# SSD scan of a hybrid decoder step: the samples' token parts read four-fold from memory on 128 rows, in place of three-fold copies turned by TensorE

## The chip, the cores and the metric

The kernel runs on one core of one Trainium2 chip. The metric is device time in microseconds of one execution of the whole program, which is one inference step of two decoder layers for 512 prompt tokens and 8 samples of 8 tokens each. An execution outside the profiler takes a little more than the span that the profile shows, since the span runs from the first to the last instruction.

## What is computed

Layer 0 is a Conformer and sliding-window attention mixer, layer 1 a Mamba-2 mixer, and each is followed by a convolutional FFN. The change lies in layer 1, in the chunked scan. Cut to what matters, the reference is:

```python
def ssd_scan(x, dt, a, bm, cm, h0):          # x: tokens, heads, 64; bm, cm: tokens, 4 groups, 128
    ...
    acum = jnp.cumsum(dtc * a.reshape(g, r), axis=2)
    decay = jnp.exp(jnp.where(causal, diff, -jnp.inf))
    cb = jnp.einsum('bclgn,bcsgn->bclsg', cc, bc)
    w_intra = (cb[..., None] * decay * dtc[:, :, None])
    y_diag = jnp.einsum('bclsgr,bcsgrp->bclgrp', w_intra, xc)
    decay_end = jnp.exp(acum[:, :, -1:] - acum)
    states = jnp.einsum('bclgn,bclgr,bclgrp->bcgrpn', bc, decay_end * dtc, xc)
    ...                                       # h = chunk_decay * h + states, over the chunks
    y_off = jnp.einsum('bclgn,bcgrpn,bclgr->bclgrp', cc, h_prev, jnp.exp(acum))
```

For the prompt there are four chunks of 128 tokens that start from a zero state. For the samples each of the 8 sequences is one chunk of 8 tokens that starts from its own state `h0`, and the new state of every sequence is an output: new state = decayed old state + (B of its 8 tokens) times (x of its 8 tokens, times `dt` and `decay_end`). That last product, for the samples, is what the change concerns.

## The kernel before

**Layout.** Activations lie channels by tokens: 576 columns, of which 512 are the prompt's and the last 64 the samples'. Every weight product is split in three (high weight times high and low activation, low weight times high activation: lines 160 to 162 in `mm3`), on halves of 288 columns. A weight block of 128 x 1024 comes by one DMA into one of three buffers `wr` (line 141), ScalarE rounds it to `wh` (line 150), VectorE forms the rest `wl` (line 151); one block feeds 48 such products. I call these products the wide products.

**Slots.** Working tiles come from a list of 48 + 11 equal slots (`S`, `free`, `NSLOT`, `EXTRA`). A tile gets the slot that has been free longest, so a new tile waits until the last user of its slot is done, whatever engine or DMA that was.

**The scan.** `mix1` runs `ssd(g)` for four groups g = 0 to 3, of eight heads and one B and one C each. I call them scan 0 to scan 3. `ssd` is a generator; `run(main, side)` interleaves its steps with weight units (gate columns z, B and C of the next group, the output projection of the group before), spread over n = 30 steps. The final order on each engine is made by a scheduler when the program is built, and from then on each engine executes its own list in order and waits where an operand or a slot isn't ready. All DMAs are issued by SyncE (queue SP), in order too.

The steps of one scan, with their lines:

- B of the prompt is turned to tokens by channels on TensorE (line 951, `btok` line 953).
- **The samples' state operands** (lines 955 to 988). B and the four x tiles of the group are copied by ScalarE into tiles `r3` in which the samples' 64 columns stand as two halves of 32, each three times over (line 958). TensorE turns them to 96 rows: two turns for B (line 966), eight for x (line 979). From B, ScalarE and VectorE make `bp` (rounded; the third copy holds the rest) and `b3` (lines 968 to 973); from x, VectorE makes `xf`, times `dd3`, a tile of `dt * decay_end` made three-fold once by a product with `sel3` (lines 923 to 928), and `x3` (lines 983 to 985). Three copies on 96 rows make one matmul yield high*high + low*high + high*low.
- C times B of each chunk, masked (`pc`, `pcs`, `cbm`, lines 991 to 999).
- x is turned to tokens by channels, times `dt`: `xdt`, four prompt chunks and one tile of the 64 sample tokens (lines 1002 to 1013).
- The chunk states (`pst`, `hst`, lines 1015 to 1029); the last goes out as `ssm_p` (line 1030).
- Then for each pair of heads t = 0 to 3: `carried` (line 1056: rows `ea2` of the cumulated decays from memory `acd`, product `py`), two `decays` (line 1044: 256 KB `acb` from `acd`, four ScalarE ops, one exponential, one VectorE product), `outputs` (line 1069: product `yp`).
- `load`, `begin` and `finish` (lines 1088 to 1123): the samples' old states `h0` come in, are multiplied by C (`pyo`) and decayed, and `finish` adds `b3` times `x3` (line 1118) and writes the new states.

Of the kernel before, what the change touches and what calls it, by code (L numbers as in the profile page):

```python
# [40 lines left out]
for _name, _w in (  # L41
    ("ident", 128), ("m32", 32), ("prot", 128), ("blk2", 2), ("amask", 256), ("smask", 2 * 192),
    ("tri", 128), ("tris", 64), ("bmat", 64), ("bsel", 8), ("selx", 256), ("selm", 128),
    ("sel3", 192), ("bsel3", 4),
):
    CV[_name] = _n
    _n += _w
# [2 lines left out]

class Builder:
    NSLOT = 48
    EXTRA = 11

    def __init__(self, nc, tc, d, stack):
        self.nc, self.tc, self.d = nc, tc, d
# [747 lines left out]
    def mix1(self):  # L804
        nc, d = self.nc, self.d
# [53 lines left out]
        W = 160  # L859
        pt = self.ps("pt")  # L860
# [12 lines left out]
        dt = self.Z("dt", W, bufs=1)  # L873
# [7 lines left out]
        for k in range(7, 0, -1):  # L881
# [12 lines left out]
        dab = self.Z("dab", 256, rows=64, bufs=1)  # L894
# [23 lines left out]
        pe = self.ps("pe")  # L918
        for bh in range(2):
            nc.tensor.matmul(pe[:, bh * 32:bh * 32 + 32], self.cv("selx", bh * P, P, 64), eas, start=True, stop=True)  # L920
        nc.vector.tensor_copy(eax, pe[:, 0:64])

        dtde, dd3 = self.Z("dtde", 32, rows=64, bufs=1), self.Z("dd3", 64, rows=96, bufs=1)
        nc.vector.tensor_tensor(dtde, dt[0:64, 128:160], de[0:64, 128:160], op=MUL)
        pe = self.ps("pe")
        for bh in range(2):
            nc.tensor.matmul(pe[0:96, bh * 32:bh * 32 + 32], self.cv("sel3", bh * 96, 96, 64), dtde, start=True, stop=True)
# [7 lines left out]
        pt = self.ps("pt")  # L935
# [7 lines left out]
        hp = lambda ap: ap.rearrange("p (h q) -> p h q", q=64)  # L943
        def ssd(g):

            bf, cf, xs = bfm.pop(g), cfm.pop(g), xss.pop(g)
            hs = lambda c: slice(c * 32 + 8 * g, c * 32 + 8 * g + 8)

            pt = self.ps("pt")
# [2 lines left out]
            btok = self.S("btok", NP)  # L952
            nc.scalar.activation(btok, pt, AF.Copy)

            r3 = []
            for a in [bf] + xs:
                r3.append(self.S("r3", 192))
                nc.scalar.activation(r3[-1].rearrange("p (b r t) -> p b r t", r=3, t=32),
                                     a[:, NP:T].rearrange("p (b t) -> p b t", t=32).unsqueeze(2).broadcast_to([P, 2, 3, 32]),
                                     AF.Copy)  # L960
            rep3 = lambda i, bh: r3[i][:, bh * 96:bh * 96 + 96]
            pt = self.ps("pt")
            b3 = []
            for bh in range(2):
                o = pt[0:96, bh * P:(bh + 1) * P]
                nc.tensor.transpose(o, rep3(0, bh), self.ident)
                bp = self.S("bp", P, F32R, rows=96)
                nc.scalar.activation(bp, o, AF.Copy)
                nc.vector.tensor_tensor(bp[64:96, :], o[64:96, :], bp[64:96, :].bitcast(F32), op=SUB)
                b3.append(self.S("b3", NP, F32R, rows=96))  # L970
                nc.vector.tensor_tensor(b3[bh].rearrange("p (b n) -> p b n", n=P),
                                        bp.bitcast(F32).unsqueeze(1).broadcast_to([96, 4, P]),
                                        self.cv("bsel3", 0, 4, 96).unsqueeze(2).broadcast_to([96, 4, P]), op=MUL)
                self.free(bp)
            x3 = []
            for bh in range(2):
                pt = self.ps("pt")
                for t in range(4):
                    nc.tensor.transpose(pt[0:96, t * P:(t + 1) * P], rep3(1 + t, bh), self.ident)
# [3 lines left out]
                x3.append(self.S("x3", NP, F32R, rows=96))  # L983
                nc.scalar.activation(x3[bh], xf, AF.Copy)
                nc.vector.tensor_tensor(x3[bh][32:64, :], xf[32:64, :], x3[bh][32:64, :].bitcast(F32), op=SUB)
                self.free(xf)
                yield
            self.free(r3)
            yield

            pc, pcs = self.ps("pc"), self.ps("pcs")
# [7 lines left out]
            nc.vector.tensor_tensor(cbm[0:64, NP:], pcs[0:64, 0:64], tris, op=MUL)  # L999
            yield  # L1000

            xdt = []
            for c in range(5):
                n = P if c < 4 else 64
                pt = self.ps("pt")
                for t in range(4):
                    nc.tensor.transpose(pt[0:n, t * P:(t + 1) * P], xs[t][:, c * P:c * P + n], self.ident)  # L1007
                o = self.S("xdt", NP, rows=n)
                nc.vector.tensor_tensor(hp(o), hp(pt[0:n, :]), dt[0:n, hs(c)].unsqueeze(2).broadcast_to([n, 8, 64]), op=MUL)
                xdt.append(o)  # L1010
                if c % 2:
                    yield
            yield

            H = []
            for c in range(4):
# [13 lines left out]
            nc.sync.dma_start(d["ssm_p"][g], H[3])  # L1030
            self.free(H.pop(), btok)
            yield

            es = self.S("es", NP, rows=64)
            nc.sync.dma_start(es.rearrange("p (h l) -> p h l", l=64),
# [228 lines left out]
def constants():  # L1264
    f = np.float32
    c = np.zeros((P, NCV), f)

    def put(name, a, i=0):
        c[:a.shape[0], CV[name] + i:CV[name] + i + a.shape[1]] = a

    put("ident", np.eye(P, dtype=f))
    prot = np.zeros((P, P), f)
    for o in (0, 64):
        for i in range(8):
            prot[o + 8 + i, o + i] = -1.0
# [12 lines left out]
    tb, tt = tok // 8, tok % 8  # L1288
    for bh in range(2):
        old = np.arange(P)[None, :] > rt[:, None]  # L1290
        new = (tb[None, :] == (bh * 4 + rb)[:, None]) & (tt[None, :] <= rt[:, None])
        put("smask", np.where(np.concatenate([old, new], 1), f(0), f(NEG)), bh * 192)
        inb = (tb[:, None] == (bh * 4 + rb)[None, :]) & (tt[:, None] == (row % 32)[None, :])
        put("selx", inb.astype(f), bh * P)
        put("selm", inb.T.astype(f), bh * 64)
        put("sel3", (tok[:, None] == bh * 32 + np.tile(np.arange(32), 3)[None, :]).astype(f), bh * 96)
# [12 lines left out]
    return c, cos, sin  # L1309
# [101 lines left out]
```

## Time and profile before

| what | value |
|---|---|
| median of 3 runs | 1567.7 us (1564.84 to 1568.19) |
| profiled execution, its own time | 1567.04 us |
| span in its profile | 1565.3 us |
| mean granted TensorE clock | 0.997 |
| weight loads (PEld) | 1471.1 us busy, 94% |
| GpSimd | 148.5 us busy, 9% |

The profile lists busy time by engine, groups of instructions by source line and operation with their mean duration, the idle time of an engine ahead of each group and what ended it, and the waits between engines. Matmuls overlap in their pipeline, so the duration of one (some 300 ns for 128 x 288) is more than what it costs in a row of them; that is read from the starts in the timeline.

### The profile page before, as it was taken

To read this page: it belongs to the slowest core of one execution; us is meant where nothing else is said; L and a number is where in the kernel's file an instruction comes from. 1 tells how busy PE (TensorE), PEld (TensorE's weight loads), DVE (VectorE), ACT (ScalarE), POOL (GpSimd) and SP (SyncE) were. 2 spreads that over 40 slices of the span, in tenths; PEclk is the share of its full clock that TensorE was granted. 3 is DMA by queue.
4 is the path that set the end of the run, shared out by engine and by line. 5 is a ranking of instruction groups with operands and counts; after the bars stand their busy time and mean duration, and the time that the engine had idled before them with its cause. 6 is when DMAs were issued, how large, how long until landed. Compare 5 with 4: busy or idle time off the path is not lost. (4 is left out here: it accounts for less than half of the span.)

```text
span 1565.3 us, 28515 instructions
## 1 busy us (share of the span) xinstructions
PE 1538.9 (98%) x11661; PEld 1471.1 (94%) x11661; DVE 1002.2 (64%) x1766; ACT 642.3 (41%) x1201; POOL 148.5 (9%) x365
## 2 busy tenths in 40 slices
PE   8999999999999999999999999999999999999999
PEld 7968799999999999997998998998999999999999
DVE  7858877563564464677796677676966643563552
ACT  6247553221222222475765655656542221221220
POOL 0026101000000000011202002002010000000000
PEclk9999999999999999999999999999999999999999
DMA  8504232222222222226345235235322222222232
GB/s 235 130 30 112 86 98 88 88 82 81 81 79 85 90 87 63 76 84 183 103 131 171 93 102 182 94 107 180 99 82 81 81 83 86 88 72 92 81 86 75
DMA packets 69361, 157.61 MB, mean 101 GB/s; under 512 B 19678, under 2 KB 24030, under 8 KB 69230
## 3 DMA queue, kind: packets, MB, share of 16 engines
q1 hardware_dynamic: 69230, 155.79, 32.5%
q8 instruction: 92, 1.51, 0.4%
q14 instruction: 39, 0.32, 0.1%
HBM read 140.55 MB, written 15.21 MB: 100 GB/s over the span
## 5 line engine op out<-in xcount | busy, mean ns | idle before, releaser
L160 PE MATMUL mm<-hh,wh 128*128 128x288 f32 (+1 forms) x2288 | 682.1, 299 | 7.3 <-ACT wh L150 6.9
L162 PE MATMUL mm<-hh,wl 128*128 128x288 f32 x2288 | 681.5, 298 | 1.0 <-DVE wl L151 1.0
L161 PE MATMUL mm<-hl,wh 128*128 128x288 f32 x2288 | 678.2, 297 | 0.0
L150 ACT ACTIVATE wh<-wr 128x1024 fp32r<-128x1024 f32 (+1 forms) x215 | 223.5, 1040 | 544.6 <-issue 270.7
L160 PEld LDWEIGHTS mm<-hh,wh 128*128 128x128 f32 (+1 forms) x2288 | 431.2, 189 | 12.1 <-ACT wh L150 7.2
L162 PEld LDWEIGHTS mm<-hh,wl 128*128 128x128 f32 x2288 | 430.6, 188 | 4.8 <-issue 2.0
L161 PEld LDWEIGHTS mm<-hl,wh 128*128 128x128 f32 x2288 | 432.0, 189 | 2.6 <-DVE hl L171 0.6
L151 DVE TENSOR_TENSOR wl<-wr,wh 128x1024 fp32r<-128x1024 f32 (+1 forms) x215 | 260.1, 1210 | 82.0 <-ACT wh L150 81.9
L161 PE MATMUL mm<-yl,wh 128*128 128x288 f32 x960 | 286.1, 298 | 0.2 <-DVE yl L171 0.2
L160 PE MATMUL mm<-yh,wh 128*128 128x288 f32 x960 | 285.3, 298 | 0.7 <-DVE x L259 0.7
L162 PE MATMUL mm<-yh,wl 128*128 128x288 f32 x960 | 283.3, 296 | 0.3 <-DVE wl L151 0.3
L160 PEld LDWEIGHTS mm<-yh,wh 128*128 128x128 f32 x960 | 180.4, 188 | 4.1 <-DVE x L259 1.8
L161 PEld LDWEIGHTS mm<-yl,wh 128*128 128x128 f32 x960 | 180.8, 188 | 2.7 <-issue 1.4
L162 PEld LDWEIGHTS mm<-yh,wl 128*128 128x128 f32 x960 | 180.4, 188 | 1.5 <-issue 0.9
L259 DVE TENSOR_TENSOR x<-x,mm 128x288 f32<-128x288 f32 x192 | 84.9, 450 | 144.2 <-PE mm L162 143.8
L304 DVE TENSOR_TENSOR gbuf<-mm,rs 128x224 f32<-128x224 f32 x44 | 17.2, 391 | 107.9 <-PE mm L162 107.9
L315 ACT ACTIVATE gsilu<-gconv,par 128x512 f32<-128x512 f32 x44 | 31.8, 723 | 115.7 <-DVE gconv L312 115.7
L312 DVE SCALAR_TENSOR_TENSOR gconv<-gbuf,par,gconv 128x592 f32<-128x592 f32 x88 | 73.1, 831 | 1.5
L325 DVE TENSOR_TENSOR gsilu<-mm,gsilu 128x288 f32<-128x288 f32 x88 | 40.0, 454 | 49.6 <-PE mm L162 49.6
L830 DVE SCALAR_TENSOR_TENSOR cconv<-cbuf,par,cconv 128x600 f32<-128x600 f32 x72 | 60.2, 840 | 11.6 <-ACT cconv L828 10.7
L1051 ACT ACTIVATE acb<-acb,ac 128x128 f32<-128x128 f32 x128 | 41.3, 390 | 46.7 <-DMA acb<-acd 29.3
L307 POOL COPY fpo<-gbuf 128x2 f32<-128x2 f32 x44 | 12.4, 283 | 473.2 <-DVE gbuf L304 473.2
(311 smaller groups left out, 1600.3 us busy)
## 6 DMA issues: line engine op xcount, KB each, us to landing
wr<-in_w_gate SPq DMA_DIRECT2D x44, 512.0 KB, 3.3
wr<-in_w_up SPq DMA_DIRECT2D x44, 512.0 KB, 3.3
wr<-in_w_in_o SPq DMA_DIRECT2D x40, 512.0 KB, 3.4
wr<-in_w_down SPq DMA_DIRECT2D x32, 448.0 KB, 3.3
wr<-in_w_down SPq DMA_DIRECT2D x16, 512.0 KB, 3.5
acb<-acd SPq DMA_DIRECT2D x32, 256.0 KB, 4.1
h<-in_h SPq DMA_DIRECT2D x32, 256.0 KB, 3.6
out_ssm_s<-h SPq DMA_DIRECT2D x32, 256.0 KB, 2.5
```

Of the source, the lines that this page charges most:

```text
L150: nc.scalar.activation(hi[:, :n], raw[:, :n], AF.Copy)
L151: nc.vector.tensor_tensor(lo[:, :n], raw[:, :n], hi[:, :n].bitcast(F32), op=SUB)
L160: nc.tensor.matmul(out, hi[:, ws], xh[:, sl], start=i == 0, stop=False)
L161: nc.tensor.matmul(out, hi[:, ws], xl[:, sl], start=False, stop=False)
L162: nc.tensor.matmul(out, lo[:, ws], xh[:, sl], start=False, stop=i == n - 1)
L259: nc.vector.tensor_tensor(self.x[m][:, sl], self.x[m][:, sl], p[:, :HB], op=ADD)
L304: nc.vector.tensor_tensor(g[:, 290:514], p[:, 0:224], rs[:, HB:NP], op=MUL)
L312: nc.vector.scalar_tensor_tensor(cv[:, :592], g[:, k:592 + k], w(k), cv[:, :592], op0=MUL, op1=ADD)
L315: nc.scalar.activation(sl[:, :NP], cv[:, :NP], AF.Silu, bias=b)
L325: nc.vector.tensor_tensor(sl[:, HALF[half]], p[:, :HB], sl[:, HALF[half]], op=MUL)
L830: nc.vector.scalar_tensor_tensor(cv[:, :600], g[:, k:600 + k], w(k), cv[:, :600], op0=MUL, op1=ADD)
L1051: nc.scalar.activation(acb[:, cs], acb[:, cs], AF.Relu, bias=ac[:, o:o + 1], scale=-1.0)
```

## The change

Ahead of the scans, `dd3`, `dtde` and their two products with the constant `sel3` go, and `da`, `dab` move from buffers of their own to slots; one slot more is made. In each scan the five `r3` copies and the ten turns to 96 rows go. In their place B's sample columns are turned once, as 64 rows, behind the turns of `btok`; ScalarE copies them to `b64`, and a DMA writes them to a DRAM tile `bx`. The sample chunk of `xdt` is now made first, is multiplied by `decay_end` (`x64`) and goes to `bx` too. Four DMAs then read 32 rows of `bx` each into 128 rows, four times over (`four`), and `bp`, `b3`, `x3` are made from these, on 128 rows, behind the chunk states and no longer ahead of them. The fourth copy is multiplied by zero (`bsel3` has rows for three), so that the sum is what it was. `run` counts 29 steps.

```diff
 class Builder:
     NSLOT = 48
-    EXTRA = 11
+    EXTRA = 12
...
-        da = self.Z("da", W, bufs=1)
+        da, dab = self.S("da", W), self.S("dab", 256, rows=64)
...
+        self.free(da, dab)
...
-        dtde, dd3 = self.Z("dtde", 32, rows=64, bufs=1), self.Z("dd3", 64, rows=96, bufs=1)
-        nc.vector.tensor_tensor(dtde, dt[0:64, 128:160], de[0:64, 128:160], op=MUL)
-        pe = self.ps("pe")
-        for bh in range(2):
-            nc.tensor.matmul(pe[0:96, bh * 32:bh * 32 + 32], self.cv("sel3", bh * 96, 96, 64), dtde, start=True, stop=True)
-        nc.vector.tensor_copy(dd3, pe[0:96, 0:64])
...
-            r3 = []
-            for a in [bf] + xs:
-                r3.append(self.S("r3", 192))
-                nc.scalar.activation(r3[-1].rearrange("p (b r t) -> p b r t", r=3, t=32), ...
...
-                nc.tensor.transpose(o, rep3(0, bh), self.ident)
...
-                    nc.tensor.transpose(pt[0:96, t * P:(t + 1) * P], rep3(1 + t, bh), self.ident)
-                xf = self.S("xf", NP, rows=96)
-                nc.vector.tensor_tensor(hp(xf), hp(pt[0:96, :]),
-                                        dd3[:, bh * 32 + 8 * g:bh * 32 + 8 * g + 8].unsqueeze(2).broadcast_to([96, 8, 64]), op=MUL)
...
+            nc.tensor.transpose(pt[0:64, 0:P], bf[:, NP:T], self.ident)
+            bx = self.dp.tile([64, NP + P], F32, name=f"bx{g}")
+            b64 = self.S("b64", P, rows=64)
+            nc.scalar.activation(b64, pt[0:64, 0:P], AF.Copy)
+            nc.sync.dma_start(bx[:, NP:], b64)
...
-            for c in range(5):
+            for c in (4, 0, 1, 2, 3):
...
+                if c == 4:
+                    x64 = self.S("x64", NP, rows=64)
+                    nc.vector.tensor_tensor(hp(x64), hp(o), de[0:64, hs(4)].unsqueeze(2).broadcast_to([64, 8, 64]), op=MUL)
+                    nc.sync.dma_start(bx[:, 0:NP], x64)
...
+            def four(name, bh, o, n):
+
+                t = self.S(name, n)
+                rows = bx[bh * 32:bh * 32 + 32, o:o + n]
+                nc.sync.dma_start(t, bass.AP(tensor=rows.tensor, offset=rows.offset, ap=[[0, 4], list(rows.ap[0]), [1, n]]))
+                return t
...
             nc.sync.dma_start(d["ssm_p"][g], H[3])
             self.free(H.pop(), btok)
             yield
+
+            b3, x3 = [], []
+            raw = [(four("bf4", bh, NP, P), four("xf4", bh, 0, NP)) for bh in range(2)]
+            yield
+            for bh, (br, xf) in enumerate(raw):
+                bp = self.S("bp", P, F32R)
+                nc.scalar.activation(bp, br, AF.Copy)
+                nc.vector.tensor_tensor(bp[64:96, :], br[64:96, :], bp[64:96, :].bitcast(F32), op=SUB)
...
+                x3.append(self.S("x3", NP, F32R))
+                nc.scalar.activation(x3[bh], xf, AF.Copy)
+                nc.vector.tensor_tensor(x3[bh][32:64, :], xf[32:64, :], x3[bh][32:64, :].bitcast(F32), op=SUB)
+                self.free(br, xf, bp)
...
-            n, k = 30, 0
+            n, k = 29, 0
```

The order of the built program shows how this moves instructions. First TensorE from the opening of scan 1 on, before; at each mark wide products are left out, in turn 16, 6, 5, 17, 5 and 6 of them. `bfm` and `cfm` are B and C, `r_...` the three-fold copies, `pt` a bank that takes turned tiles.

```order
L951 MATMUL pt<-ident,bfm 128x128 x4
L966 MATMUL pt<-ident,r_8779 96x128
...
L979 MATMUL pt<-ident,r_8781 96x128
L979 MATMUL pt<-ident,r_8783 96x128
...
L979 MATMUL pt<-ident,r_8785 96x128
...
L966 MATMUL pt<-ident,r_8779 96x128
...
L979 MATMUL pt<-ident,r_8781 96x128
L979 MATMUL pt<-ident,r_8783 96x128
L979 MATMUL pt<-ident,r_8785 96x128
...
L979 MATMUL pt<-ident,r_8787 96x128 x2
...
L994 MATMUL pc<-cfm,bfm 128x128 x4
```

The ten turns to 96 rows come in five visits among the wide products, and one that stands beside the turns of B. Behind these rows come the turns of x, in four visits (8, 4, 4 and 4), and the first chunk state `pst` stands 90 wide products behind the opening. The same place now; the marks stand for 10, 9, 4, 9, 6 and 1 wide products, and `xs` is x.

```order
L944 MATMUL pt<-ident,bfm 128x128 x4
L949 MATMUL pt<-ident,bfm 64x128
...
L960 MATMUL pc<-cfm,bfm 128x128 x4
L961 MATMUL pcs<-cfm,bfm 64x64
...
L973 MATMUL pt<-ident,xs 64x128 x3
...
L973 MATMUL pt<-ident,xs 128x128 x3
...
L973 MATMUL pt<-ident,xs 128x128
L973 MATMUL pt<-ident,xs 64x128
...
L973 MATMUL pt<-ident,xs 128x128 x4
...
L973 MATMUL pt<-ident,xs 128x128 x4
```

The turns to 96 rows are gone, the turns of x come earlier and in six visits (the last, of 4, ten wide products further on), and the first chunk state stands 63 wide products behind the opening where it stood 90 behind it.

Second, the DMA queue SP at the same scan, before, from the weight loads ahead of it on (`h_...` are old states, `ea_...` and `acb` rows of decays from memory).

```order
L141 DMA wr<-in_w_in_o 128x1024 x2
L1092 DMA h_9027<-in_h 128x512
L1092 DMA h_9029<-in_h 128x512
L1092 DMA h_9031<-in_h 128x512
L1060 DMA ea_9033<-acd 64x384 x2
L1047 DMA acb<-acd 128x512
L1035 DMA es<-acd 64x8x64
L1092 DMA h_9025<-in_h 128x512
L141 DMA wr<-in_w_in_o 128x1024
```

And now, with the two writes to `bx` and the four reads of it:

```order
L141 DMA wr<-in_w_in_o 128x1024 x2
L953 DMA bx_8764<-b_8765 64x128
L990 DMA bf_8968<-bx_8764 128x1x128
L990 DMA bf_8972<-bx_8764 128x1x128
L1029 DMA es<-acd 64x8x64
L980 DMA bx_8764<-x_8785 64x512
L990 DMA xf_8970<-bx_8764 128x1x512
L990 DMA xf_8974<-bx_8764 128x1x512
L1086 DMA h_8998<-in_h 128x512
L1041 DMA acb<-acd 128x512
L1054 DMA ea_9006<-acd 64x384 x2
L1008 DMA out_ssm_p<-hst 128x512
```

Six DMAs have been put ahead of the old states and of the first `acb`, two of them wait for a write to land that stands just before them, and no weight load stands between the `acb` loads of the first pair any longer (the next one comes five rows behind `out_ssm_p`).

More of the change, by code (lines that the diff above doesn't have):

```diff
@@ L43 @@
     ("tri", 128), ("tris", 64), ("bmat", 64), ("bsel", 8), ("selx", 256), ("selm", 128),
-    ("sel3", 192), ("bsel3", 4),
+    ("bsel3", 4),
 ):
@@ L953, in ssd @@
             nc.scalar.activation(btok, pt, AF.Copy)
-            r3 = []
-            for a in [bf] + xs:
-                r3.append(self.S("r3", 192))
[L958 to L961, printed above, removed]
-            pt = self.ps("pt")
@@ L963, in ssd @@
[L963 to L979, printed above, removed]
-                xf = self.S("xf", NP, rows=96)
-                nc.vector.tensor_tensor(hp(xf), hp(pt[0:96, :]),
-                                        dd3[:, bh * 32 + 8 * g:bh * 32 + 8 * g + 8].unsqueeze(2).broadcast_to([96, 8, 64]), op=MUL)
[L983 to L987, printed above, removed]
@@ L988, in ssd @@
-            self.free(r3)
+            pt = self.ps("pt")
+            nc.tensor.transpose(pt[0:64, 0:P], bf[:, NP:T], self.ident)
[3 more added lines that the diff above has]
+            nc.sync.dma_start(bx[:, NP:], b64)
+            self.free(b64)
             yield
@@ L1000, in ssd @@
             yield
-            xdt = []
-            for c in range(5):
+            xdt = [None] * 5
+            for c in (4, 0, 1, 2, 3):
                 n = P if c < 4 else 64
@@ L1009, in ssd @@
                 nc.vector.tensor_tensor(hp(o), hp(pt[0:n, :]), dt[0:n, hs(c)].unsqueeze(2).broadcast_to([n, 8, 64]), op=MUL)
-                xdt.append(o)
-                if c % 2:
+                xdt[c] = o
+                if c == 4:
+                    x64 = self.S("x64", NP, rows=64)
+                    nc.vector.tensor_tensor(hp(x64), hp(o), de[0:64, hs(4)].unsqueeze(2).broadcast_to([64, 8, 64]), op=MUL)
+                    nc.sync.dma_start(bx[:, 0:NP], x64)
+                    self.free(x64)
+                elif c % 2:
                     yield
             yield
+            def four(name, bh, o, n):
[3 more added lines that the diff above has]
+                return t
             H = []
@@ L1032, in ssd @@
             yield
+            b3, x3 = [], []
[5 more added lines that the diff above has]
+                nc.vector.tensor_tensor(bp[64:96, :], br[64:96, :], bp[64:96, :].bitcast(F32), op=SUB)
+                b3.append(self.S("b3", NP, F32R))
+                nc.vector.tensor_tensor(b3[bh].rearrange("p (b n) -> p b n", n=P),
+                                        bp.bitcast(F32).unsqueeze(1).broadcast_to([P, 4, P]),
+                                        self.cv("bsel3", 0, 4).unsqueeze(2).broadcast_to([P, 4, P]), op=MUL)
+                x3.append(self.S("x3", NP, F32R))
+                nc.scalar.activation(x3[bh], xf, AF.Copy)
+                nc.vector.tensor_tensor(x3[bh][32:64, :], xf[32:64, :], x3[bh][32:64, :].bitcast(F32), op=SUB)
+                self.free(br, xf, bp)
             es = self.S("es", NP, rows=64)
```

2 lines of the change are left out of this document (removed).

## The prediction, made before the changed kernel was run

> **What bounds the kernel now.** I read the page's busy times first, then the windows of the four scans, then the waits of TensorE alone, then the places in the timeline to which they point.
>
> ```profile
> PE 1538.9 (98%) x11661; PEld 1471.1 (94%) x11661; DVE 1002.2 (64%) x1766; ACT 642.3 (41%) x1201; POOL 148.5 (9%) x365
> ```
>
> TensorE (PE) is busy for 98% of the span, the next engine for 64%. So what counts is work on TensorE and the gaps on TensorE. Work on VectorE, ScalarE or a queue costs only where TensorE comes to wait for it.
>
> ```profile
> 400.00:440.00 40.00, 40.00 (x304) 40.00 (x303) 22.81 (x36) 10.87 (x15) 2.02 (x10) 1.00 0.28 91
> 699.00:766.00 67.00, 63.11 (x483) 56.04 (x482) 50.00 (x81) 41.32 (x93) 11.68 (x20) 0.97 0.50 152
> 796.00:870.00 74.00, 71.51 (x546) 64.67 (x546) 57.21 (x98) 38.91 (x84) 10.87 (x21) 0.98 0.53 159
> 917.00:985.00 68.00, 65.83 (x510) 58.77 (x510) 54.60 (x90) 35.11 (x72) 11.22 (x17) 1.00 0.54 165
> 1030.00:1098.00 68.00, 66.07 (x515) 58.91 (x514) 49.46 (x81) 38.03 (x83) 10.01 (x10) 1.00 0.49 159
> ```
>
> The columns are the stretch in us, its length, busy time of PE, PEld, DVE, ACT and POOL, the granted clock, the DMA share, GB/s. The first row is a stretch of wide products: 304 in 40.00 us, so one costs 0.1316 us and nothing is idle. The others are scans 0 to 3: TensorE lacks 3.9, 2.5, 2.2 and 1.9 us, and in two of them the clock is below 1. The DMA share of about half leaves room for transfers. These are the stages in which the change lies, so its worth is read here.
>
> ```profile
> PE yp L1077 <- DVE acb L1053: 5.9, 4, 1.9
> PE pst L1118 <- DVE ea L1066: 2.7, 1, 2.7
> PE pt L979 <- ACT r L958: 1.1, 1, 1.1
> PE pst L1118 <- DVE h L1119: 0.4, 1, 0.4
> PE pt L979 <- DVE bp L969: 0.2, 1, 0.2
> ```
>
> The columns are who waits for whom, the total, how often, the longest. In the scans TensorE waits for 5.9 + 2.7 + 1.1 + 0.4 + 0.2 = 10.3 us. Only 1.3 of that stands at the turns that go (L979). The rest stands at `yp` and at the new states, behind the place of the change.
>
> **The change part by part.** First, the work on TensorE that is removed.
>
> ```profile
> L979 PE MATMUL pt<-ident,r 128*96 128x128 f32 x32 | 6.1, 287 | 1.4 <-ACT r L958 1.1 <-DVE bp L969 0.2
> L966 PE MATMUL pt<-ident,r 128*96 128x128 f32 x8 | 2.4, 294 | 0.0
> L927 PE MATMUL pe<-dtde,cst 64*96 64x32 f32 x4 | 0.5, 251 | 0.0
> ```
>
> That is 40 turns, ten for each scan, and L927 once. Their busy times overlap with their neighbours', so I price them by the starts around them, in scan 0:
>
> ```profile
> 702.32 0.29 PE L161 MATMUL mm<-hl,wh 128*128 128x288 f32 x1
> 702.53 0.32 PE L966 MATMUL pt<-ident,r 128*96 128x128 f32 x1
> 702.60 0.38 PE L162 MATMUL mm<-hh,wl 128*128 128x288 f32 x1
> 702.82 0.29 PE L160 MATMUL mm<-hh,wh 128*128 128x288 f32 x1
> ...
> 704.82 0.30 PE L160 MATMUL mm<-hh,wh 128*128 128x288 f32 x1
> 705.08 0.53 PE L979 MATMUL pt<-ident,r 128*96 128x128 f32 x3
> 705.37 0.38 PE L161 MATMUL mm<-hl,wh 128*128 128x288 f32 x1
> 705.58 0.29 PE L162 MATMUL mm<-hh,wl 128*128 128x288 f32 x1
> ```
>
> A visit with one turn: from 702.32 to 702.82 two wide products pass, 0.50 - 2 x 0.132 = 0.24 us. A visit with three: from 704.82 to 705.58, 0.76 - 0.26 = 0.50. So a visit costs about 0.11 and each turn in it 0.13. Scan 1 has five visits and one turn beside others: 5 x 0.11 + 10 x 0.13 = 1.85. Counted only to the start of the first product behind them, the two visits cost 0.28 - 0.13 = 0.15 and 0.55 - 0.13 = 0.42, which makes 0.135 for a turn and almost nothing for a visit: 1.4. So a scan lies between 1.4 and 1.85. Four scans: 5.6 to 7.4, plus L927 at most 0.5. **Added**: one turn beside those of B (0.13) and two more visits (0.22) for the turns of x, 4 x 0.35 = 1.4, bounded by 1.0 and 3.0, since three visits more stand in the other scans and a visit of which the bank isn't free costs more. The new `pst` products contract over 128 rows in place of 96, with as many columns; they have the same number and I price that at nothing. Net on TensorE: -2.6 to -6.9, **I take -4.5 us**.
>
> Second, the gaps and their consequence for the clock.
>
> ```profile
> 737.15 0.50 PE L1118 MATMUL pst<-x,b 96*128 96x512 f32 x1 [2.73 <-DVE ea L1066]
> 845.70 1.09 PE L1077 MATMUL yp<-acb,xdt 128*64 128x128 f32 x16 [1.71 <-DVE acb L1053]
> ```
>
> ```profile
> 738.00:740.00 2.00, 2.00 (x10) 0.51 0.34 131
> 740.00:742.00 2.00, 2.00 (x11) 0.64 0.80 233
> 846.00:848.00 2.00, 2.00 (x24) 0.82 0.72 282
> 848.00:850.00 2.00, 2.00 (x10) 0.50 0.01 4
> 850.00:852.00 2.00, 2.00 (x15) 0.83 0.00 0
> 1080.00:1084.00 4.00, 3.87 (x35) 1.00 0.26 100
> ```
>
> These windows show TensorE alone; the third number from the right is the granted clock. Behind the gap of 2.73 it is 0.51 and 0.64: 2 x 0.49 + 2 x 0.36 = 1.7 us lost. Behind the gap of 1.71 it is 0.82, 0.50, 0.83: 0.36 + 1.00 + 0.34 = 1.7 us lost. The last row follows the longest `yp` wait, 1.9 in the list above, and the clock stays 1.00. So a gap of about 2 us sometimes costs 1.7 more. The waits and their clock are 10.3 + 3.4 = 13.7 us that the new order may keep, lose or replace.
>
> [...]
>
> Third, what the new order puts in place of these waits. The chain that ends at `yp` in scan 1 is, now:
>
> ```profile
> 794.36 0.60 PE L951 MATMUL pt<-ident,bfm 128*128 128x128 f32 x4
> ...
> 819.84 0.34 SPq L1030 DMA_DIRECT2D out_ssm_p<-hst  x1
> 823.94 0.32 SPq L1047 DMA_DIRECT2D acb<-acd  x1
> 824.00 1.09 PE L1077 MATMUL yp<-acb,xdt 128*64 128x128 f32 x16
> 827.83 1.29 ACT L1051 ACTIVATE acb<-acb,ac 128x128 f32<-128x128 f32 x4 [0.89 <-DMA acb<-acd]
> 830.56 1.09 PE L1077 MATMUL yp<-acb,xdt 128*64 128x128 f32 x16 [0.73 <-DVE acb L1053]
> ```
>
> ```profile
> acb<-acd SPq DMA_DIRECT2D x32, 256.0 KB, 4.1
> out_ssm_p<-hst SPq DMA_DIRECT2D x4, 256.0 KB, 3.8
> ```
>
> S is the opening, 794.36. The last state is sent at S+25.5 and lands 3.8 later; an `acb` load that takes its slot is issued at S+29.6; ScalarE starts on it 3.9 later and `yp` follows 2.7 after that, at S+36.2, after a wait of 0.73. It serves the second pair of heads. In the new order of SP the `acb` behind `out_ssm_p` serves a product of the **first** pair, which is wanted sooner. Both ends of that chain move. The end of the states: some 24 VectorE operations stand from the opening to there; the scan's row has 98 in 57.21, 0.584 each, so 14.0 us from S+7.5, at which the first turned x tile is there (32 wide products, 4.2 us, and some 3 us of turns and C products ahead of it): the send at S+21.5, the load at about S+25, `yp` ready at S+25 + 3.9 + 2.7 = S+31.6. TensorE's arrival: before, it came to the first `yp` at S+29.6 behind 139 wide products (18.3 us), so 11.3 us was other work. Now 148 stand ahead (19.5), and other work is 11.3 less 1.85, plus 0.35, plus about 0.6 for `py` that moved ahead: 10.4, so S+29.9. A wait of some 1.7 us. For the smaller waits behind it I add 0.8: 2.5 us in scan 1. Scan 2 has the same order: 2.5. In scan 0 no `acb` of the first pair stands behind `out_ssm_p`, and the decay rows `ea` on which the 2.73 hung are loaded earlier: 0.5. In scan 3 two `acb` loads wait for slots that `yp` of the first pair frees, so a whole chain of 4.1 + 2.7 lies behind it, partly covered by wide products: 3.0. In all 8.5, an estimate between 0 (wide products cover all) and 20 (each of 8 pairs waits 2.5). Of the clock I keep one loss, 1.7, between 0 and 4 x 1.7 = 6.8.
>
> Fourth, the **bounce through memory**. SP gets two writes and four reads more for each scan.
>
> ```profile
> out_ssm_s<-h SPq DMA_DIRECT2D x32, 256.0 KB, 2.5
> L1047 SPq DMA_DIRECT2D acb<-acd x4: 319/330/525, 804.1 to 823.9; - x4
> ```
>
> The nearest row of a write says 2.5 us from issue to landing, for 256 KB where these have 32 and 128. Queued behind the read that waits for it are, in scan 1, the row load `es`, four old states, the first `acb` and the `ea`. Two holds of 2.5 and six issues of 0.33 (the mean in the second row) are 7.0 us. The first `acb` was issued at 804.1; with 4.1 to land and 2.7 to `yp` it could have been used at 810.9, and was used at 824.00: 13.1 us of slack, less than 7.0 leaves over. I take nothing, between 0 and 4 x 5 us. `b3` and `x3` are wanted only at L1118, behind two `yp`, so the reads have still more time. On ScalarE and VectorE the copies, `xf` and `dd3` go and `x64` comes; both are at most 80% busy in each scan (54.60 of 68.00), so I price that at nothing too, and its bounds are in those of the waits. The added slot and the 29 steps shift wide products by a row here and there: nothing, within the same bounds.
>
> **Sum**, against the profiled execution's own 1567.04 (0.7 us below the median shown, inside the spread of the runs): 1567.0 - 4.5 - 13.7 + 8.5 + 1.7 = **1559.0 us**.
>
> **The rivals.** (a) *The waits stay as large as they are*, since a load always stands last at `yp`: only the direct work counts, 1567.0 - 4.5 = 1562.5. For it speaks that `acb` and not the turns ended most waits; against it, the 2.73 at `ea`, whose load now stands far ahead. (b) *New waits eat the gain*: the waits of scans 1 and 2 come out at 3.5 and that of scan 3 at 5, and two of them cost clock: 0.5 + 3.5 + 3.5 + 5 + 3.4 = 15.9, and the net on TensorE is the small end, 2.6: 1567.0 - 2.6 - 13.7 + 15.9 = 1566.6, no change. (c) *Slower: SP is held by the bounce.* The queue is in order, and a read of `bx` waits until the write has landed. This decides from the point at which the hold ahead of the first `acb` exceeds the 13.1 us of slack. A hold of 18 would delay the first `yp` of each scan by 5 and cost clock: 4 x (5 + 1.7) = 26.8; 1567.0 - 4.5 - 13.7 + 26.8 = 1575.6. Against it stands the 2.5 of the write row; for it, that no row shows a read that waits for a write directly ahead of it, and that the `x64` write itself waits for VectorE, which is 77% busy in scan 1. (d) *It doesn't do what it says*: if the turns lay wholly beside weight loads, removing them would give nothing; the 0.24 and 0.50 above exclude it.
>
> **How the numbers follow.** Forecast, 1559 with its own range 1554 to 1563: 0.52. Rival (a): 0.18. Rival (b): 0.18. Rival (c): 0.12. A measurement of this kernel can tell about 0.2%, 3 us. Faster is the forecast and (a): 0.70; same is (b): 0.18; slower is (c): 0.12. The range takes in (a) and (b); below, it reaches to where new waits are about 3 us in all, 1567.0 - 4.5 - 13.7 + 3 = 1552. Above, it ends at 1568 and leaves out (c).
>
> **What would show it.** In the profile of the changed kernel L979 and L966 are gone and the turns of x are in six visits or so; PE busy time falls by some 3 to 6 us; the waits list has 5 to 12 us in the scans, most at `yp` behind `acb`, none at `ea`; the `acb` behind `out_ssm_p` is issued near S+25 in scans 1 and 2. Reads of `bx` land 3 to 4 us after their writes and nobody on TensorE waits for `b3` or `x3`. Waits of over 15 us in the scans, a wait at the products of line 1112, or a clock below 1 behind more than two gaps would make the prediction wrong.

## The result, and the profile after

| kernel | median | runs |
|---|---|---|
| before | 1567.32 us | 1564.84 to 1568.19, 4 runs |
| changed | 1603.01 us | 1600.91 to 1603.19, 4 runs |

The ratio is 1.0224, with a 95% interval of 1.0208 to 1.0239: slower by some 35 us where 8 us faster was forecast. The page of the changed kernel begins so (the span, then busy time, share of the span and instructions of each engine):

```profile
span 1600.8 us, 28465 instructions
...
PE 1547.8 (97%) x11621; PEld 1478.6 (92%) x11621; DVE 1000.3 (62%) x1760; ACT 634.3 (40%) x1183; POOL 151.8 (9%) x365
```

The span grew by 35.5 us. TensorE (PE) has 40 instructions fewer, and yet is busy 8.9 us longer; its idle time, span less busy, went from 26.4 to 53.0 us. One way to be busy for longer with less work is a lower clock: from 836.45 to 840.04, where 0.50 is granted, fifteen wide products take 0.24 us each, against 0.13 at 1.00. So the next view is the windows of TensorE alone (stretch, length, PE busy with its count, granted clock, DMA share, GB/s), with the gaps ahead of them in its timeline (start, duration, instruction, and in brackets the idle time before it and what ended it):

```profile
727.08 1.65 PE L1058 MATMUL py<-cfm,hst 128*128 128x128 f32 x6 [4.98 <-DVE hst L1004]
835.42 0.69 PE L1071 MATMUL yp<-acb,xdt 128*64 128x128 f32 x2 [5.40 <-DVE acb L1047]
963.75 0.69 PE L1071 MATMUL yp<-acb,xdt 128*64 128x128 f32 x2 [5.46 <-DVE acb L1047]
1107.62 2.83 PE L1071 MATMUL yp<-acb,xdt 128*64 128x128 f32 x24 [3.88 <-DVE acb L1047]
```

```profile
836.00:840.00 4.00, 4.00 (x17) 0.50 0.11 44
964.00:968.00 4.00, 4.00 (x17) 0.50 0.17 69
1108.00:1112.00 4.00, 4.00 (x30) 0.50 0.04 11
```

Each scan has a gap of 4 to 5.5 us, and behind each the clock stands at 0.50, in the windows shown and in scan 0 from 726 to 734; the work lost there, estimated as (1 - clock) times busy time, 2.4 to 3.0 us for each, makes some 5 to 6 us at half the clock. Four smaller gaps of 2.2 to 2.5 us cost 1.6 to 1.7 us each. I summed the same product over windows of 2 us from 690 to 1140: by this estimate 3.4 us of TensorE's work were lost to the clock before, 17.6 after. That closes the account: idle time +26.6, clock +14.2, and the rest, TensorE's own work, is 8.9 - 14.2 = -5.3; together 35.5.

The waits of TensorE in the stretch of the scans (who waits for whom, total, times, longest):

```profile
PE yp L1071 <- DVE acb L1047: 25.5, 9, 5.5
PE py L1058 <- DVE hst L1004: 5.0, 1, 5.0
PE pyo L1093 <- DMA h<-in_h: 2.8, 2, 1.4
```

The list of before had 10.3 us in the scans. Now `yp` alone has 25.5, and in scan 0 a chunk state `hst` is late, for which TensorE nowhere waited before. The chain behind the gap of 5.40 in scan 1 (opening at 801.0) runs over three engines. First SyncE (start, duration), then ScalarE and VectorE:

```profile
810.62 0.49 SPq L980 DMA_DIRECT2D bx<-x  x1
812.95 1.12 SPq L990 DMA_DIRECT2D xf<-bx  x2
814.16 2.82 SPq L1086 DMA_DIRECT2D h<-in_h  x4
817.91 0.33 SPq L1041 DMA_DIRECT2D acb<-acd  x1
818.71 1.38 SPq L1054 DMA_DIRECT2D ea<-acd  x2
824.14 0.33 SPq L1041 DMA_DIRECT2D acb<-acd  x1
```

```profile
819.69 0.63 ACT L1024 ACTIVATE x<-xf 128x512 fp32r<-128x512 f32 x1 [4.24 <-DMA xf<-bx]
824.21 0.63 ACT L1024 ACTIVATE x<-xf 128x512 fp32r<-128x512 f32 x1 [3.88 <-DMA xf<-bx]
827.96 1.28 ACT L1045 ACTIVATE acb<-acb,ac 128x128 f32<-128x128 f32 x4 [3.12 <-DMA acb<-acd]
...
834.03 1.13 ACT L1046 ACTIVATE acb<-acb 128x512 f32<-128x512 f32 x2
```

```profile
834.68 0.69 DVE L1047 TENSOR_TENSOR acb<-acb,cbm 128x512 f32<-128x512 f32 x1 [0.34 <-ACT acb L1046]
```

The write of `x64` is issued at 810.62 and its two readers at 812.95, so the write took some 2.3 us. The reads are wanted by the two conversions of line 1024, which start at 819.69 and 824.21, at once when the data is there: 6.7 us after the first issue and 10.7 us after the second, at 813.5. A plain load of the same 256 KB, an old state, landed in 3.6 in the kernel before. ScalarE stands at these conversions for 8.1 us, and the four operations of the first decay come behind them in its list. But the conversions are not what ends last here: the first decay waits 3.12 us more, for its `acb` load. That one was issued at 817.91 and is there at 827.9, 10 us after its issue, where the median was 4.1 before. The second `acb` is issued only at 824.14, when the second read has landed. It is the eighth DMA behind that read on SyncE, whose list of waits has 9.4 us at `acb` loads for the reads; in the kernel before, each of the 422 DMAs of SyncE for which the trace gives both times is issued after the eighth ahead of it has landed, the closest 0.02 us after. Scan 2 looks the same. In scan 0 it is the conversions that end last: VectorE stands idle for 5.63 us at the rest of one, with the chunk state `hst` behind it in its list:

```profile
722.84 0.96 DVE L1025 TENSOR_TENSOR x<-xf,x 32x512 fp32r<-32x512 f32 x1 [5.63 <-ACT x L1024]
```

So a slow read comes to TensorE on two ways: engines stand at the conversions (8.1 us of ScalarE in scan 1), and loads that are issued behind the read land late too (10 us for the first `acb`).

Two readings suggested themselves first: the queue is held by the bounce, or the conversions wait for reads that are slow. Why are the reads slow? Scan 3 shows them almost by themselves, since no old states are loaded beside them there (windows of 1 us, TensorE alone; the last two numbers are the DMA share and GB/s):

```profile
1073.00:1074.00 1.00, 1.00 (x9) 1.00 0.22 25
1074.00:1075.00 1.00, 1.00 (x10) 1.00 0.27 106
```

```profile
1071.81 1.13 SPq L990 DMA_DIRECT2D xf<-bx  x2
...
1078.05 0.63 ACT L1024 ACTIVATE x<-xf 128x512 fp32r<-128x512 f32 x1 [5.55 <-DMA xf<-bx]
...
1081.48 0.63 ACT L1024 ACTIVATE x<-xf 128x512 fp32r<-128x512 f32 x1 [2.79 <-DMA xf<-bx]
```

With hardly more than these reads under way the DMA share is about a quarter, and they take 6.2 and 9.1 us. The packets in the trace give the same picture: from 1073.2 to 1075.6 four are under way at once for 84% of the time and never more than six; from 1077 to 1079, with other loads beside, it is 15 in the mean. Four is also the size of the outermost step of the read's address pattern, the copies, and that suggests theory D below.

### The profile page after: what moved, and what is told of

It reads as the page before. It is cut to its first block, busy times and chain, and to the rows that moved or that the text cites. A ratio compares the mean times of both kernels' runs of the same rounds, so it can differ in the third digit from the quotient of the medians.

```text
span 1600.8 us, 28465 instructions
## 1 busy us (share of the span) xinstructions
PE 1547.8 (97%) x11621; PEld 1478.6 (92%) x11621; DVE 1000.3 (62%) x1760; ACT 634.3 (40%) x1183; POOL 151.8 (9%) x365
## 4 chain that ended last, share of the span: by engine, by line
PE 81%; DVE 6%; DMA 4%; ACT 3%; issue 1%; SPq 0%; POOL 0%; ACTq 0%; DVEq 0%; POOLq 0%
PE mm L162 24%; PE mm L161 24%; PE mm L160 24%; DMA acb<-acd 2%; PE yp L1071 1%; PE mm L563 1%; ACT acb L1045 1%; DMA ea<-acd 1%; DMA out_ssm_s<-h 1%; PE pr L193 1%; ACT wh L150 1%; DVE ca L443 1%; DVE wl L151 1%; PE pt L182 0%; PE pst L1112 0%
## 5 line engine op out<-in xcount | busy, mean ns | idle before, releaser
L160 PE MATMUL mm<-yh,wh 128*128 128x288 f32 x960 | 289.0, 301 | 0.8 <-DVE x L259 0.8
L1099 POOL TENSOR_TENSOR h<-h,cds 128x512 f32<-128x512 f32 x32 | 37.8, 1213 | 176.4 <-PE pyo L1093 176.3
```

The lines of the kernel that those rows point to most:

```text
L160: nc.tensor.matmul(out, hi[:, ws], xh[:, sl], start=i == 0, stop=False)
L1099: nc.gpsimd.tensor_tensor(hp(h0[bh][b4]), hp(h0[bh][b4]), cds[:, b * 32 + 8 * g:b * 32 + 8 * g + 8].unsqueeze(2).broadcast_to([P, 8, 64]), ...
```

## The experiments

The theories: **Q**, SyncE is held; **C**, the conversions stand in ScalarE's and VectorE's lists ahead of states and decays and wait for the reads; **O**, the new order of TensorE, or the place of the block, costs by itself; **B**, slot and step count cost by themselves; then, for why the reads are late, **D**, the outermost step of four keeps a read at a quarter of the DMA share; **L**, they share the engines with other loads; **R**, reading the same rows again is slow. All times are medians, all ratios are to the kernel before, measured beside it.

### The bounce on another queue

```diff
-            nc.sync.dma_start(bx[:, NP:], b64)
+            nc.gpsimd.dma_start(bx[:, NP:], b64)
...
-                    nc.sync.dma_start(bx[:, 0:NP], x64)
+                    nc.gpsimd.dma_start(bx[:, 0:NP], x64)
...
-                nc.sync.dma_start(t, bass.AP(
+                nc.gpsimd.dma_start(t, bass.AP(
```

> The changed kernel with its six DMAs of each scan (two writes to bx, four reads) issued by GpSimd, in place of SyncE; the rows of TensorE and the rest of SyncE's stand in the same order. Theory Q (SyncE is held: its list is in order, a read waits for the write ahead of it, and each DMA waits until the eighth before it has landed, so that the old states and the first acb loads come late and in one burst): old states are issued some 8 us earlier, the waits at yp and py fall by more than half, 1570 to 1585 us. Theory C (ScalarE and VectorE meet the conversions of b3 and x3 ahead of the states and the decays, and wait there for the reads to land): the reads still wait for their writes, the waits stay, 1595 to 1606 us. Theory O (the new order of TensorE itself): no change, 1600 to 1606 us.

1600.88 us, ratio 1.0216 (1.0193 to 1.0238): nothing came back. The list of DMAs by kind (KB each, median us from issue to landing); the same list for those issued from 811 to 819 us, beside and behind the two large reads of scan 1; SyncE's row for the second `acb` there; and the waits of ScalarE and TensorE:

```profile
h<-in_h SPq DMA_DIRECT2D x32, 256.0 KB, 3.5
...
xf<-bx POOLq DMA_DIRECT2D x8, 256.0 KB, 9.2
```

```profile
h<-in_h SPq DMA_DIRECT2D x4, 256.0 KB, 8.8
xf<-bx POOLq DMA_DIRECT2D x2, 256.0 KB, 8.8
acb<-acd SPq DMA_DIRECT2D x2, 256.0 KB, 10.1
```

```profile
817.89 0.58 SPq L1041 DMA_DIRECT2D acb<-acd  x1
```

```profile
ACT x L1024 <- DMA xf<-bx: 30.6, 8, 6.4
```

```profile
PE yp L1071 <- DVE acb L1047: 25.8, 9, 5.6
```

The second `acb` is issued 6 us earlier than in the changed kernel (817.89 against 824.14), so SyncE was held there; but ScalarE still waits 30.6 us for the reads (30.3 in the changed kernel) and `yp` waits as long. Nothing was won since the loads behind the reads land late even from a queue of their own: 8.8 and 10.1 us in scan 1, where the kernel before has 2.8 and 3.7 for its loads there. So the loss does not hang on SyncE being held; with the split reads below SyncE waits for the writes nearly as long, and nothing is lost. The read lands after 9.2 us where the median old state of the same size takes 3.5, on this queue too.

### The conversions later

```diff
-            for bh, (br, xf) in enumerate(raw):
-                bp = self.S("bp", P, F32R)
...
-                self.free(br, xf, bp)
...
+                if t == 1:
+                    for bh, (br, xf) in enumerate(raw):
+                        bp = self.S("bp", P, F32R)
...
+                        self.free(br, xf, bp)
                 if t % 2:
                     yield from finish(t // 2, last)
```

> The changed kernel with the conversions to b3 and x3 written ahead of the first finish, behind the outputs of the second pair of heads; writes and reads of bx stay where they are written. Theory C (conversions that wait for the reads stand ahead of states and decays on ScalarE and VectorE): the waits of py and yp in scans 0 to 2 go down to about 1 to 2 us each scan, 1565 to 1580 us. Theory Q (SyncE is held): at most a third of the loss comes back, 1590 to 1603 us. Theory O: 1598 to 1606 us.

1579.35 us, ratio 1.0073 (1.0051 to 1.0095): some two thirds of the loss came back. The waits of TensorE:

```profile
PE yp L1058 <- DVE acb L1034: 12.0, 6, 3.4
PE pst L1099 <- DVE h L1100: 6.9, 3, 3.4
```

The wait at `yp` is halved, that of `py` for a chunk state is gone, and a smaller one at the new states has come. So C has a part, but 12.6 us over the kernel before are left, and the size of the part is not shown: with 11 slots and 30 steps the same move wins nothing (1588.7 us against 1587.09, both below). What is left can be seen on ScalarE in scan 1, where the `acb` load is now issued 0.6 us behind the second read:

```profile
803.78 0.41 SPq L1028 DMA_DIRECT2D acb<-acd  x1
813.56 1.28 ACT L1032 ACTIVATE acb<-acb,ac 128x128 f32<-128x128 f32 x4 [8.29 <-issue]
```

The profile names no releaser for these 8.29 us; the semaphore on which the decay waits is that of this load, which is then there 9.7 us after its issue.

### The block's place without the bounce

```diff
-            pt = self.ps("pt")
-            b3 = []
...
-            self.free(r3)
-            yield
...
             nc.sync.dma_start(d["ssm_p"][g], H[3])
             self.free(H.pop(), btok)
             yield
+            pt = self.ps("pt")
+            b3 = []
...
+            self.free(r3)
+            yield
```

> The kernel before, with its own two-and-eight turns to 96 rows, but the block from the turns to b3 and x3 written behind the chunk states, where the change has it; no bounce through memory. If the place of the block and the order that comes of it are what costs (theory O), it is slower than before by 15 us or more, 1582 to 1605 us. If the bounce costs (theories Q and C), it stays within 1562 to 1575 us.

1572.44 us, ratio 1.0033 (1.0021 to 1.0045), some 5 us: the place has a price, but a sixth of the loss. The place is not the cause, and the split reads below lose nothing with the block in its new place.

### Slot and steps

```diff
-    EXTRA = 12
+    EXTRA = 11
...
-            n, k = 29, 0
+            n, k = 30, 0
```

> The changed kernel with 11 slots more and 30 steps, as before, in place of 12 and 29. If the slot and the step count move the loss about (theory B, bookkeeping), it is 1575 to 1590 us; if the bounce costs (theories Q and C), within 8 us of the changed kernel, 1595 to 1611 us.

1587.09 us, ratio 1.0123 (1.0105 to 1.014). I had not thought these two numbers worth anything, and they move 16 us, into the range of B. The waits of ScalarE for the reads (29.0 us) and of `yp` (22.4 us) stay in kind:

```profile
PE yp L1071 <- DVE acb L1047: 22.4, 10, 4.1
```

This leaves open whether B acts by itself or only changes where the slow reads hurt; three runs below take it up again.

### Four reads of 32 rows in place of one of four copies

```diff
-                nc.sync.dma_start(t, bass.AP(tensor=rows.tensor, offset=rows.offset, ap=[[0, 4], list(rows.ap[0]), [1, n]]))
+                for r in range(4):
+                    nc.sync.dma_start(t[32 * r:32 * r + 32, :], rows)
```

> The changed kernel with each four-fold read made as four reads of 32 rows, one for each copy, in place of one read whose outermost step is the four copies; same bytes, 16 issues more for each scan on SyncE. Theory D (one read with an outermost step of four runs on a quarter of the DMA engines, and so lands after 6 to 11 us; ScalarE and VectorE meet the conversions in order and wait for it): the two reads of x land within 4 to 6 us of their issue, ScalarE's wait for them falls from 30 us to below 15, and the time to 1575 to 1592 us. Theory L (the reads are late since the old states and decays share the DMA engines with them): landing stays at 6 to 11 us and the time within 8 us of the changed kernel's, 1595 to 1611.

1563.52 us, ratio 0.998 (0.9971 to 0.9989): the same bytes with 16 reads for a scan in place of 4 (12 issues more, not the 16 of the expectation), and the whole loss is gone and a little more, below the 1575 at which the range of theory D began. Its page, its waits and its DMAs:

```profile
PE 1533.8 (98%) x11621; PEld 1465.5 (94%) x11621; DVE 1001.3 (64%) x1760; ACT 636.9 (41%) x1185; POOL 152.2 (10%) x365
```

```profile
PE yp L1072 <- DVE acb L1048: 11.2, 8, 2.4
```

```profile
ACT x L1025 <- DMA xf<-bx: 2.0, 3, 1.0
```

```profile
xf<-bx SPq DMA_DIRECT2D x32, 64.0 KB, 1.9
```

A read of 32 rows lands in 1.9 us, and ScalarE waits 2.0 us for them in the scans where it waited 30.3, though the old states are loaded beside them as before: L falls. SyncE still stands at the reads until the writes have landed, 13.1 us in the scans (9.0 for B, 4.1 for x) in place of 15.4, so this hold costs little. The build set the other instructions into a somewhat different order, so this run alone doesn't separate D from the order; the next pair does.

### The address pattern alone, in the kernel before

```diff
-                    nc.sync.dma_start(h0[bh][b4], d["h0"][4 * bh + b4, g])
+                    src = d["h0"][4 * bh + b4, g]
+                    nc.sync.dma_start(h0[bh][b4], bass.AP(tensor=src.tensor, offset=src.offset, ap=[[0, 4], [NP, 32], [1, NP]]))
```

The second run of the pair has `[[0, 16], [NP, 8], [1, NP]]`. Every engine's list is that of the kernel before, instruction for instruction.

> The kernel before, in the same order on every engine, with its 32 loads of old states made as four-fold reads: the first 32 rows of each state four times, outermost step of four, the same 256 KB (the old states are then partly wrong ones). Nothing waits for a write here. Theory D (an outermost step of four keeps a DMA on a quarter of the DMA engines): an old state lands 8 us or more after its issue in place of 3.6, at a DMA share of about a quarter while such loads run alone, and the kernel is slower by 10 us or more. Theory R (reading the same rows of memory again is what is slow): the same here, and the same in the next run too.

> The kernel before, in the same order, with its 32 loads of old states made as sixteen-fold reads: the first 8 rows sixteen times, outermost step of sixteen, the same 256 KB (the old states are then partly wrong ones). Theory D: landing within 3 to 4.5 us as before, and the time within 4 us of the kernel before. Theory R: landing of 8 us or more and slower by 10 us or more.

With four copies outermost 1609.1 us, ratio 1.028 (1.0266 to 1.0294); with sixteen 1565.74 us, ratio 1.0002 (0.9992 to 1.0011). Two of the four-fold run's longest waits; then two places in which it loads old states, SyncE's rows with the windows of TensorE (DMA share and GB/s last) and the product that waits for the second four loads; then the sixteen-fold run's DMA row:

```profile
PE yp L1077 <- DVE acb L1053: 14.6, 5, 4.0
PE pst L1020 <- ACT hst L1023: 7.1, 2, 5.4
```

```profile
812.06 3.69 SPq L1093 DMA_DIRECT2D h<-in_h  x3
...
814.00:815.00 1.00, 1.00 (x9) 1.00 0.25 96
816.00:817.00 1.00, 1.00 (x10) 1.00 0.25 96
...
1097.61 2.83 SPq L1093 DMA_DIRECT2D h<-in_h  x4
...
1114.71 1.94 PE L1100 MATMUL pyo<-h,cfm 128*32 128x512 f32 x8 [8.19 <-DMA h<-in_h]
```

```profile
h<-in_h SPq DMA_DIRECT2D x32, 256.0 KB, 3.9
```

Same bytes, same order, same re-reading of rows (even more of it in the second): only the outermost step differs, and it makes 43 us. D is shown, R falls. From 814 to 817 us hardly anything but the three loads is under way (the next one is issued at 815.85), and the share is a quarter (0.25), as D has it. The profile gives no times to landing for the four-fold run; but the product at 1114.71 starts when its old states are there, 14 us or more after the last of them was issued (by 1100.4), so "8 us or more" holds.

So reads with an outermost step of four ran at a quarter of the DMA share in both kernels: 0.22 to 0.27 with the reads of `bx` nearly alone in the changed kernel, and 0.25 with the four-fold old states alone. That a quarter of the engines carries such a read, as the expectations put it, is an inference from this share and from the four packets at a time in scan 3; the profile doesn't show single engines. The pattern stood in the diff, and my prediction didn't weigh it.

### Both together, and slot and steps again

The late conversions with split reads:

> The conversions written ahead of the first finish, and the reads split in four as well. Theory D with C: in this place the reads have landed before they are wanted, so the split gives nothing more: 1574 to 1584 us. If slow reads also hold up the other transfers through shared DMA engines, it is faster than that, 1562 to 1574.

1565.27 us, ratio 0.9987 (0.9977 to 0.9996). So with quick reads the place of the conversions no longer matters (1563.52 with them early); and the late conversions with slow reads, 1579.35, lost another 14 us. Of the two expectations the second holds: slow reads hold up other transfers (through shared engines or not, the profile doesn't show). The first `acb` behind the large reads of scan 1, which took 9.7 us there, lands in 3.9 here, and the wait at the new states falls from 6.9 us to 1.2.

The late conversions with slow reads, 11 slots and 30 steps:

> The conversions written ahead of the first finish, with 11 slots and 30 steps. Theory C alone (slot and steps only moved the waits behind the reads about): within 5 us of the run with 12 and 29, 1574 to 1584. If slot and steps act by themselves (theory B): some 16 us off, 1560 to 1567.

1588.7 us, ratio 1.0142 (1.0128 to 1.0156). Both expectations missed: slower by 9 us, not equal and not faster. ScalarE's list of waits no longer names the reads, but it has 30.8 us for `acb` loads (22.8, and at most 4.5 at once, in the run above):

```profile
ACT acb L1032 <- DMA acb<-acd: 30.8, 9, 9.5
PE yp L1058 <- DVE acb L1034: 20.4, 7, 4.7
PE py L1045 <- DVE hst L1004: 6.3, 1, 6.3
```

The kernel before with 29 steps:

> The kernel before with 29 steps in place of 30, nothing else. Theory B (the spreading of the weight units costs by itself): slower by 5 us or more, 1572 to 1585. Otherwise within 4 us of the kernel before, 1563 to 1571.

1570.15 us, ratio 1.0022 (1.0012 to 1.0032), 3 us: within the 4 us, so the spreading alone costs little there.

The split reads with 11 slots and 30 steps:

> The changed kernel with split reads and with 11 slots and 30 steps. If slot and steps only moved about the waits for slow reads, it is within 5 us of the run with 12 and 29, 1559 to 1568; if they act by themselves (theory B), it is off by some 16 us.

1555.95 us, ratio 0.9933 (0.992 to 0.9947). This version beats both kernels, by some 10 us the one before. Both expectations missed: it is 8 us off the run with 12 and 29, not within 5 and not some 16. Its waits:

```profile
PE yp L1072 <- DVE acb L1048: 5.5, 6, 1.5
PE pyo L1094 <- DMA h<-in_h: 2.0, 3, 1.2
```

No gap in the scans is over 1.5 us, and the sum of lost clock in the scans is 0. Going from 12 slots and 29 steps to 11 and 30, then, is worth -16 and +9 us with slow reads and -8 with quick ones, and from 29 to 30 steps alone -3 in the kernel before: with slow reads the two numbers have no sign of their own. They change the order that the build makes, and with it which waits fall where; which of the two does it, and by which step, stays open. Splitting the reads, in contrast, wins in each of the three pairs: 1603.01 to 1563.52, 1579.35 to 1565.27, and 1587.09 to 1555.95.

## Why the prediction was wrong, point by point

- **What bounds the kernel**: right. The loss is gaps on TensorE and the clock behind them, and two of the signs named for a wrong prediction came: waits of over 15 us in the scans, and lost clock behind more than two gaps.
- **The work taken from TensorE**, -4.5 us (-2.6 to -6.9): right. The account above leaves -5.3, and in the run with split reads, where the waits are small, it is -5.0 (busy time 1533.8 less 3.3 of lost clock, against 1538.9 less 3.4).
- **Waits and clock of before**, 13.7 us that may be kept, lost or replaced: right as a size; the 2.73 at `ea` did go, as forecast.
- **The new waits**, 8.5 us: mis-sized where the reads enter. In scan 3 the forecast was 3.0 and 3.9 was measured, though nothing in the forecast knew of the slow reads there, so this nearness shows nothing. The gaps of scans 0, 1 and 2 sum to 9.6, 9.5 and 10.5 us where 0.5, 2.5 and 2.5 were forecast. In scan 1 TensorE came to the first `yp` at S+29.0 (forecast S+29.9), but `yp` was ready at S+34.4 and not at S+31.6.
- **The clock**, 1.7 us kept: 17.6. The gaps are longer and there are more of them: 0.50 was granted behind each of the four of 4 to 5.5 us, and the four of 2.2 to 2.5 us cost 1.6 to 1.7 each.
- **The bounce, "I take nothing": this is the step that failed.** It priced the write by a row for a write (2.5 us; 2.3 was measured) and the hold of SyncE by the issues, and both came out about right and of no consequence, as the runs with the other queue and with split reads show. It never priced the *read*. Its size was taken as that of any load, "3 to 4 us after their writes", while the address pattern, copies outermost, was in the diff; 6 to 11 us were measured. And it said that the reads "have still more time", since `b3` and `x3` are wanted late on TensorE. What counted was not who wants the result but what stands behind the read: in the lists of ScalarE and VectorE, chunk states and decays behind the conversions (ScalarE waits 30.3 us for the reads, and VectorE stood idle for 5.63 with a chunk state behind); and among the transfers, the `acb` loads, which landed after some 10 us in place of 4.1. The forecast's own sum for the first `acb` of scan 1 held at the issue (7.2 us later than before, 7.0 forecast) and failed at the "4.1 to land". How the loss divides between the two ways is not shown.
- **Slot and 29 steps, nothing**: wrong. 3 to 16 us, of either sign with slow reads.
- **The rivals**: (c) had the side, by luck, and its time was too small (1575.6): its mechanism, SyncE held by the write, was not the cause. The rival that was missing is a slow read at which ScalarE and VectorE stand, and behind which the loads land late.

With the reads split, the terms of the forecast can be compared one by one: TensorE's own work -5.0 (forecast -4.5), waits of 11.2 us at `yp` (8.5 in all), none at `ea` (as forecast), 3.3 us of lost clock (1.7), and 1563.52 us in place of 1559.0. With 11 slots and 30 steps it is 1555.95; that the forecast lies between the two is no confirmation, since the 8 us between them belong to no term of it.

## What to carry to other kernels

Price each new DMA by its own address pattern, on both sides, and not by the bytes of its nearest neighbour: look at its outermost step (over the 32 loads of old states a step of 4 took 43 us more than one of 16), and check it by the DMA share while it runs nearly alone (0.25 there). When data is wanted late, ask which engine first touches it, what else stands behind that instruction in its list, and which transfers are issued behind the slow one. Small counts such as a slot or a step can move the time by as much as the edit that was meant (here 16, 9 and 8 us, against a forecast gain of 8), so compare a change in more than one such setting before its size is believed.

## What the runs showed of the hardware that was not expected

- The same 256 KB in the same order cost 43 us more over 32 loads (1609.1 against 1565.74) when its outermost step was 4 and not 16. On GpSimd's queue the read was as slow, 9.2 us to landing.
- Loads beside and behind the four-fold reads landed late, even those of another queue: with the reads on GpSimd's queue, old states and `acb` issued on SyncE's beside and behind them took 8.8 and 10.1 us in scan 1, against 2.8 and 3.7 in the kernel before. Why they are late is not shown: the profile doesn't show single engines.
- The gaps on TensorE cost about half as much again in clock here: of the loss of 35.5 us, 26.6 is idle time and 14.2, by the estimate above, lost clock (0.50 behind the gaps of 5.40, 5.46 and 3.88), against the 5.3 gained.
